# Reading the moving operand backwards and the weights in steps of two, in a two-layer decoder trunk

## The chip, the core and the metric

The kernel runs on one core of one Trainium2 chip. The metric is the device time of one execution in microseconds. Before the change two runs gave 976.68 and 978.26 us, with a median of 977.47 us.

## What is computed

The reference is a decoder trunk of two layers over 256 tokens of width 1024, in float32. Cut to what matters here:

```python
def swiglu(h, w_in, w_out):
    g, u = jnp.split(h @ w_in, 2, axis=-1)
    return (jax.nn.silu(g) * u) @ w_out

for layer in range(2):
    if layer == 1:
        k_sh, v_sh, F_sh = shared_kv(x, ...)              # h @ kv_w, gates
    sh1, sc1, g1, sh2, sc2, g2, sh3, sc3, g3 = split(c_act @ ada_w[layer] + ada_b[layer], 9)
    h = modulate(rms_norm(x, norm_g[layer, 0]), sh1, sc1)
    x = x + 0.5 * g1 * swiglu(h, ffn_w_in[layer, 0], ffn_w_out[layer, 0])
    h = modulate(rms_norm(x, norm_g[layer, 1]), sh2, sc2)
    mix = diff_attention(h, ...) if layer == 0 else forgetting_attention(h, ..., k_sh, v_sh, F_sh)
    x = x + g2 * mix
    h = modulate(rms_norm(x, norm_g[layer, 2]), sh3, sc3)
    x = x + 0.5 * g3 * swiglu(h, ffn_w_in[layer, 1], ffn_w_out[layer, 1])
return rms_norm(x, final_g)
```

A feed-forward block takes the 256 tokens through 2 x 2816 hidden columns and back. There are four of these blocks, and they hold most of the arithmetic; the two attentions, their projections and one shared key and value projection hold the rest.

## The kernel before, in words

Activations are kept transposed: a tile has 128 features on the partitions and the 256 tokens along the free axis. Every large product is made in a split form. A float32 operand is written as a high part of type float32r (tiles `HH`, `hidh`, `wh`) and a low part, the rest (tiles `HL`, `hidl`, `wl`). The helper `mm3` then issues three TensorE matmuls into one PSUM sum: high weights with high activations, low weights with high activations, high weights with low activations. In `mm3` the weight block of 128x128 is the **stationary** operand, which TensorE loads ahead of the matmul, and the activations of 256 tokens are the **moving** operand, which it streams. So each matmul has a weight load of its own, and writes 256 columns of float32 into PSUM. Where a bias column rides along, a matmul has 258 columns.

Weights arrive from HBM as a stream of pieces of up to 1024 columns. SyncE issues a DMA into a `raw` tile, ScalarE copies it to `wh`, VectorE subtracts to get `wl`. A piece of 1024 columns holds eight blocks, that is 24 matmuls. `take` hands out the pieces in order, and its inner `blk(c, w)` gives the two views, high and low, of the block that starts at column `c`.

Names of the products that go through `mm3`: `pf`, `pg`, `pu` (into a feed-forward block; in the first block, four of its eleven column groups are `pf`), `po` (out of it), `pqk`, `pk` (query and key projections), `pw` (attention output), and with 258 columns `lp`, `lg`, `lu`, `lq` (the first products after a new residual, whose normalisation is applied later). Not through `mm3` go: the value projections `pv`, where the weights are the moving operand with 512 columns and the activations are stationary; the last feed-forward output, also called `po`, where weights of 256 columns move and `hidh` or `hidl` is stationary; the forget gate `pzf`; and the small float32 products and transposes of the attention.

The order of instructions on every engine is fixed when the program is built. `InOrder` wraps each engine, keeps an estimate of when each tile is ready, and the background work (ScalarE copies, VectorE subtractions, and the VectorE reductions of the `ada` matrices) is put in where that estimate leaves room. The estimate knows a tile by its name and, for some tiles, by the offset of the view.

One detail of the weight tiles matters below. `wh` and `wl` are 1088 columns wide, and a table `shift` makes a few pieces begin 16 or 32 columns (64 or 128 bytes) later in their tile: the first piece of one group of products in each feed-forward block, and all pieces of the last output projection. All others begin at column 0.

Of the kernel before, what the change touches and what calls it, by code (L numbers as in the profile page):

```python
# [17 lines left out]
P = 128  # L18
D = 1024
S = 256  # L20
NC = D // P
HD = 64
AH = 8
# [27 lines left out]
V_ADAB = 65  # L51


class InOrder:


# [18 lines left out]
    def __getattr__(self, name):  # L75
        f = getattr(self.engine, name)

        def call(*args, **kw):
            aps = [v for v in (*args, *kw.values()) if hasattr(v, "tensor")]
            if aps:  # L80
                names = [(v.tensor.name, v.offset if v.tensor.name[:2] in ("HH", "HL", "x_", "mo") else 0) for v in aps]
                cost = self.fixed + self.rate * math.prod(aps[0].shape[1:])
                if aps[1:] and aps[1].dtype == F32:
                    cost *= {"matmul": 4, "transpose": 2}.get(name, 1)
                start = max(InOrder.ready.get(n, 0.0) for n in names[name == "matmul":])
                if self.fill and not self.busy:
                    self.busy = True
                    self.fill(start)
                    self.busy = False
                self.t = max(self.t, start) + cost  # L90
                if name == "dma_start":
                    InOrder.ready[names[0]] = self.t + 2.0
                else:
                    outs = [names[0]] + ([(kw["accum_out"].tensor.name, 0)] if kw.get("accum_out") is not None else [])
                    for n in outs:
                        InOrder.ready[n] = self.t + 0.06
            else:
                self.t += 1.3
            return self.tc.keep_in_program_order(f(*args, **kw))  # L99
        return call  # L100
# [3 lines left out]
def trunk(ctx, tc, a, out):  # L104
# [125 lines left out]
    stream = []  # L230
# [4 lines left out]
    def add_ffn(l, i):  # L235
        if (l, i) == (0, 0):
            stream.extend((a["win0"][k], K0 * 512, 1024) for k in range(NC))
        n = 2 * (NG - K0 if (l, i) == (0, 0) else NG)
        stream.extend((a["win"][win0_of(l, i) + u], 2048, 1024) for u in range(n))
        if (l, i) == (1, 1):  # L240
            for u in range(4):
                stream.extend((a["wlast"][u, :, c:c + n], n, step)
                              for c, n, step in ((0, 2048, 1024), (2048, 2048, 1024), (4096, 1536, 768)))
        else:
            stream.extend((a["wout"][(2 * l + i) * 16 + u], 11 * P, 768) for u in range(16))
# [11 lines left out]
    stream += [(a["wo"][u], 2048, 1024) for u in range(4, 8)]  # L257
    add_ffn(1, 1)

    pieces = [(src, c0, min(step, ncols - c0), c0 + step >= ncols)  # L260
              for src, ncols, step in stream for c0 in range(0, ncols, step)]

    shift = {}
    for (l, i), j in ((0, 0), K0), ((0, 1), 1), ((1, 0), 0), ((1, 1), 1):
# [7 lines left out]
    raws, his, los = [], [], []  # L272
# [52 lines left out]
    def take(src, split=False):  # L325

        u = taken[0]
        assert stream[u][0].tensor.name.endswith(src), (stream[u][0].tensor.name, src)
        p0 = done[0] = begun[0]
        while len(used) < p0:  # L330
            used.append(pe.t)
        while len(his) < p0 + 2:
            cp_part()
        while len(los) < p0 + 2:
            sub_part()
        taken[0] += 1
        begun[0] += 2
        step = stream[u][2]

        def blk(c, w=P):  # L340
            o = c % step
            if c >= step and not split and done[0] == p0:
                done[0] = p0 + 1
                used.append(pe.t)
            return his[p0 + c // step][:, o:o + w], los[p0 + c // step][:, o:o + w]
        return blk

    def work(cols):

        credit[0] = min(CREDIT, credit[0] + pace[0] * 2 * cols / 2048)  # L350
        if mode[0] != "hold":
            bg()
# [51 lines left out]

    def mm3(ps, w, xx, first, last):
        (wh, wl), (xh, xl) = w, xx
        mm(ps, wh, xh, start=first, stop=False, skip_group_check=True)
        mm(ps, wl, xh, start=False, stop=False, skip_group_check=True)
        mm(ps, wh, xl, start=False, stop=last, skip_group_check=True)
        work(P)  # L410


    HH = cp_.tile([P, NC, SP_], F32R, name="HH")
    HL = cp_.tile([P, NC, SP_], F32R, name="HL")
# [492 lines left out]
    for k in range(0, NC, 2):  # L907
# [3 lines left out]
        if k % 4:  # L911
            i = k // 4
# [481 lines left out]
def _layout(x, c, ada_w, ada_b, norm_g, ffn_w_in, ffn_w_out, a_w_qkv, a_w_o, a_lambda,  # L1394
            a_subln_g, rel_bias, kv_ada_w, kv_ada_b, kv_norm_g, kv_w, fgate_w, fgate_b,
            b_w_q, b_w_o, final_g):
    cat = np.concatenate
    r = {}
    r["x"] = x[0].T.reshape(NC, P, S).transpose(1, 0, 2)
    r["c"] = c.reshape(1, D)  # L1400

    def cols(v):
        return v.reshape(-1, P).T

    def pairs(m):
        m = m.reshape(-1, P, D)
        return m

    ada, adab = [], []

    def unit(b0, b1, v0, v1):
        ada.append(cat([b0, b1], axis=1))
        adab.extend([v0, v1])

    def ada_sec(wT, bb, sec):
        return wT[sec * D:(sec + 1) * D].reshape(NC, P, D), bb[sec * D:(sec + 1) * D].reshape(NC, P)

    def mod_pair(wT, bb, s_sc, s_sh):
        w1, b1 = ada_sec(wT, bb, s_sc)
        w0, b0 = ada_sec(wT, bb, s_sh)  # L1420
        for j in range(NC):
            unit(w1[j], w0[j], b1[j], b0[j])

    for l in range(2):
        if l == 1:
            mod_pair(kv_ada_w.T, kv_ada_b, 1, 0)
        wT = ada_w[l].T
        for s in range(3):
            mod_pair(wT, ada_b[l], 3 * s + 1, 3 * s)
            w, b = ada_sec(wT, ada_b[l], 3 * s + 2)  # L1430
            for j in range(0, NC, 2):
                unit(w[j], w[j + 1], b[j], b[j + 1])
    r["ada"] = np.stack(ada)
    r["vecs"] = cat([cols(norm_g), cols(kv_norm_g), cols(final_g), cols(a_subln_g), np.stack(adab, axis=1)], axis=1)

    def gu(w):
        g = w[:, :FF].reshape(NC, P, NG, 256)
        u = w[:, FF:].reshape(NC, P, NG, 256)
        return cat([g, u], axis=3)

    win = []
    for l in range(2):
        for i in range(2):
            w = gu(ffn_w_in[l, i])
            if (l, i) == (0, 0):
                r["win0"] = w[:, :, :K0].reshape(NC, P, K0 * 512)
                w = w[:, :, K0:]
            n = w.shape[2]
            win.append(w.reshape(2, 4, P, n, 512).transpose(3, 0, 2, 1, 4).reshape(2 * n, P, 2048))
    r["win"] = cat(win, axis=0)  # L1450
    w = ffn_w_out.reshape(4, FF, D)
    r["wout"] = w[:3].reshape(3, 2, 11, P, NC, P).transpose(0, 4, 1, 3, 2, 5).reshape(48, P, 11 * P)
    r["wlast"] = w[3].reshape(22, P, 4, 256).transpose(2, 1, 0, 3).reshape(4, P, 22 * 256)
    r["fin"] = final_g.reshape(1, D)

    def vmat(w):
        return w.reshape(2, 4, P, 2, 512).transpose(3, 0, 2, 1, 4).reshape(4, P, 2048)

    def kouter(w):
        return w.reshape(4, 2, P, D).transpose(0, 2, 1, 3).reshape(4, P, 2048)  # L1460

    def bpairs(w):
        return w.reshape(NC, P, 4, 256).transpose(2, 1, 0, 3).reshape(4, P, 2048)

    w = a_w_qkv[0]
    qk = cat([w[:, :D].reshape(NC, P, AH, P), w[:, D:2 * D].reshape(NC, P, AH, P)], axis=3)
    r["wqk"] = qk.transpose(2, 1, 0, 3).reshape(AH, P, 2048)
    r["wv"] = vmat(w[:, 2 * D:])
    r["wo"] = cat([kouter(a_w_o[0]), kouter(b_w_o[0])], axis=0)
    r["wkk"] = bpairs(kv_w[:, :D])  # L1470
    r["wkv"] = vmat(kv_w[:, D:])
    r["wq"] = bpairs(b_w_q[0])
    r["fgw"] = fgate_w.reshape(NC, P, BH).transpose(1, 0, 2)
    r["fgb"] = fgate_b.reshape(BH, 1)
    k = _constants()

    def rows(v):
        return np.concatenate([v, np.zeros((P - v.shape[0], v.shape[1]), np.float32)], axis=0)

    r["misc"] = cat([k["ident"], k["cmask"], k["ub"], rows(k["hot"]),  # L1480
                     np.broadcast_to(k["umask"], (P, 383)), rows(rel_bias),
                     np.broadcast_to(a_lambda.reshape(1, 4 * HD), (P, 4 * HD))], axis=1)
    return {k: np.ascontiguousarray(v) for k, v in r.items()}
# [16 lines left out]
```

## Time and profile before

| | before |
|---|---|
| runs | 976.68 and 978.26 us, median 977.47 us |
| span of the profiled execution, first to last instruction | 974.4 us |
| TensorE matmuls | busy 963.7 us, 8124 of them |
| TensorE weight loads | busy 939.9 us, 8124 of them |
| VectorE | busy 818.5 us |
| ScalarE | busy 552.4 us |
| HBM read | 264.75 MB, 274 GB/s over the span |

The span lies 3.07 us under the median of the runs: 2.3 to 3.9 us of a run are outside the first and the last instruction. Of the rows, two readings need care. The busy time of one matmul, 276 ns at 256 columns, is not what it costs: matmuls are pipelined, and the next one starts long before. What a matmul costs in a row of them is the distance between starts, which follows from the length of an unbroken piece of the chain divided by its count. And a weight load runs while the matmul before it streams, so the two TensorE rows lie on top of each other.

### The profile page before, as it was taken

To read this page: it belongs to the slowest core of one execution; us is meant where nothing else is said; L and a number is where in the kernel's file an instruction comes from. 1 tells how busy PE (TensorE), PEld (TensorE's weight loads), DVE (VectorE), ACT (ScalarE), POOL (GpSimd) and SP (SyncE) were. 2 spreads that over 40 slices of the span, in tenths; PEclk is the share of its full clock that TensorE was granted. 3 is DMA by queue.
4 is the path that set the end of the run, shared out by engine and by line. 5 is a ranking of instruction groups with operands and counts; after the bars stand their busy time and mean duration, and the time that the engine had idled before them with its cause. 6 is when DMAs were issued, how large, how long until landed. Compare 5 with 4: busy or idle time off the path is not lost.

```text
span 974.4 us, 20491 instructions
## 1 busy us (share of the span) xinstructions
PE 963.7 (99%) x8124; PEld 939.9 (96%) x8124; DVE 818.5 (84%) x1372; ACT 552.4 (57%) x902; POOL 54.6 (6%) x94
## 2 busy tenths in 40 slices
PE   8999999999999999999999999999999999999997
PEld 6999999998999999999997999999998999999997
DVE  7989979989999999878899989989977699555575
ACT  5466545566787645455576554445567576455432
POOL 0000200000112000000000000000011014300000
PEclk9999999999999999999999999999999999999999
DMA  9988999967776699888959899998885337978651
GB/s 360 415 352 279 332 372 339 345 225 272 293 239 232 209 381 370 293 287 314 329 179 370 308 338 337 345 314 319 297 278 174 104 109 228 266 149 276 185 152 44
DMA packets 69473, 268.22 MB, mean 275 GB/s; under 512 B 9417, under 2 KB 10225, under 8 KB 59266
## 3 DMA queue, kind: packets, MB, share of 16 engines
q1 hardware_dynamic: 66016, 259.69, 76.1%
q0 software_dynamic: 3072, 6.92, 2.5%
q8 instruction: 63, 1.03, 0.4%
q10 hardware_dynamic: 290, 0.32, 0.1%
q14 instruction: 32, 0.26, 0.1%
HBM read 264.75 MB, written 2.66 MB: 274 GB/s over the span
## 4 chain that ended last, share of the span: by engine, by line
PE 97%; DVE 1%; DMA 1%; ACT 0%; issue 0%; SPq 0%; DVEq 0%; ACTq 0%
PE po L99 25%; PE pg L99 21%; PE pu L99 21%; PE pf L99 5%; PE pv L99 5%; PE pw L99 4%; PE lp L99 4%; PE pqk L99 3%; PE wb L99 1%; PE lq L99 1%; PE lu L99 1%; PE lg L99 1%; PE pk L99 1%; PE sb L99 1%; DMA ada<-in_ada 1%; PE s L99 1%
## 5 line engine op out<-in xcount | busy, mean ns | idle before, releaser
L99 ACT CAST wh<-raw 128x1024 fp32r<-128x1024 f32 (+1 forms) x360 | 347.3, 975 | 210.8 <-PE pu L99 82.0
L99 DVE TENSOR_TENSOR wl<-raw,wh 128x1024 fp32r<-128x1024 f32 (+1 forms) x360 | 398.6, 1126 | 70.9 <-ACT sg L99 20.3
L99 DVE CUSTOM_DVE_ANT_0 ada<-ada,cact,vecs 128x1024 f32<-128x1024 f32 x160 | 203.6, 1279 | 0.4 <-DMA ada<-in_ada 0.4
L99 PE MATMUL pg<-HH,wh 128*128 128x256 f32 x608 | 168.0, 276 | 0.0
L99 PE MATMUL pg<-HH,wl 128*128 128x256 f32 x608 | 167.9, 276 | 0.0
L99 PE MATMUL pu<-HH,wh 128*128 128x256 f32 x608 | 167.9, 276 | 0.0
L99 PE MATMUL pu<-HL,wh 128*128 128x256 f32 x608 | 167.9, 276 | 0.0
L99 PE MATMUL pg<-HL,wh 128*128 128x256 f32 x608 | 167.9, 276 | 0.0
L99 PE MATMUL pu<-HH,wl 128*128 128x256 f32 x608 | 167.9, 276 | 0.0
L99 PE MATMUL po<-hidh,wh 128*128 128x256 f32 x528 | 145.7, 276 | 0.0
L99 PE MATMUL po<-hidh,wl 128*128 128x256 f32 x528 | 145.7, 276 | 0.0
L99 PE MATMUL po<-hidl,wh 128*128 128x256 f32 x528 | 145.7, 276 | 0.0
L99 PEld LDWEIGHTS pg<-HH,wh 128*128 128x128 f32 x608 | 114.1, 188 | 0.7 <-issue 0.6
L99 PEld LDWEIGHTS pg<-HH,wl 128*128 128x128 f32 x608 | 114.1, 188 | 0.0
L99 PEld LDWEIGHTS pu<-HH,wh 128*128 128x128 f32 x608 | 114.1, 188 | 0.0
L99 PEld LDWEIGHTS pg<-HL,wh 128*128 128x128 f32 x608 | 114.1, 188 | 0.0
L99 PEld LDWEIGHTS pu<-HL,wh 128*128 128x128 f32 x608 | 114.1, 188 | 0.0
L99 PEld LDWEIGHTS pu<-HH,wl 128*128 128x128 f32 x608 | 114.1, 188 | 0.0
L99 PEld LDWEIGHTS po<-hidh,wh 128*128 128x128 f32 x528 | 99.1, 188 | 0.0
L99 PEld LDWEIGHTS po<-hidl,wh 128*128 128x128 f32 x528 | 99.1, 188 | 0.0
L99 PEld LDWEIGHTS po<-hidh,wl 128*128 128x128 f32 x528 | 99.1, 188 | 0.0
L99 ACT CAST hidh<-hf 128x512 fp32r<-128x512 f32 x44 | 27.3, 621 | 40.5 <-DVE hf L99 40.4
(226 smaller groups left out, 1848.4 us busy)
## 6 DMA issues: line engine op xcount, KB each, us to landing
raw<-in_win SPq DMA_DIRECT2D x176, 512.0 KB, 6.8
ada<-in_ada SPq DMA_DIRECT2D x79, 1024.0 KB, 7.2
raw<-in_wout SPq DMA_DIRECT2D x48, 384.0 KB, 5.3
raw<-in_wout SPq DMA_DIRECT2D x48, 320.0 KB, 5.5
raw<-in_wqk SPq DMA_DIRECT2D x16, 512.0 KB, 5.8
raw<-in_wo SPq DMA_DIRECT2D x16, 512.0 KB, 5.8
raw<-in_wlast SPq DMA_DIRECT2D x16, 512.0 KB, 4.5
raw<-in_wv SPq DMA_DIRECT2D x8, 512.0 KB, 7.2
```

Of the source, the lines that this page charges most:

```text
L99: return self.tc.keep_in_program_order(f(*args, **kw))
```

## The change

`mm3` turns three views around: the moving operand, high and low, is read from the last column to the first, and the output is written from the last to the first, so each token's sum lands where it did. The stationary blocks of `mm3` are read with a step of two elements: on the host, pairs of neighbouring blocks of 128 columns are interleaved element by element, and `blk` hands out the even or the odd columns of a stretch of 256. Where a block has no partner in its piece (the last of eleven in each half of a `po` column, since 11 blocks are odd), it stays whole, with step one. Products outside `mm3` are as before, and so are the layouts of `wv`, `wkv` and `wlast`. `lowest` keeps the estimator's names of turned views equal to those of the plain ones.

```diff
+def lowest(v):
+    return v.offset + sum(step * (n - 1) for step, n in v.ap[1:] if step < 0)
+
+def turned(v):
+    return v[:, ::-1]
...
+    stream = [(src, ncols, step, lambda i, n=ncols, s=step: min(s, n - i * s)) for src, ncols, step in stream]
...
         def blk(c, w=P):
             o = c % step
...
+            if w == P:
+                o, n = o // 256 * 256, o // P % 2
+                if o + 256 <= stream[u][3](c // step):
+                    return tuple(t[p0 + c // step][:, o + n:o + 256:2] for t in (his, los))
+                o += n * P
             return his[p0 + c // step][:, o:o + w], los[p0 + c // step][:, o:o + w]
...
     def mm3(ps, w, xx, first, last):
         (wh, wl), (xh, xl) = w, xx
+        ps, xh, xl = turned(ps), turned(xh), turned(xl)
         mm(ps, wh, xh, start=first, stop=False, skip_group_check=True)
         mm(ps, wl, xh, start=False, stop=False, skip_group_check=True)
         mm(ps, wh, xl, start=False, stop=last, skip_group_check=True)
...
+    def mixed(w):
+        return np.swapaxes(w.reshape(w.shape[:-1] + (w.shape[-1] // 256, 2, P)), -1, -2).reshape(w.shape)
...
-        return cat([g, u], axis=3)
+        return mixed(cat([g, u], axis=3))
...
-    r["wqk"] = qk.transpose(2, 1, 0, 3).reshape(AH, P, 2048)
+    r["wqk"] = mixed(qk.transpose(2, 1, 0, 3).reshape(AH, P, 2048))
```

The other layouts that `mm3` uses (`win`, `wout`, `wo`, `wkk`, `wq`) are wrapped in `mixed` in the same way.

No instruction moves: on all five engines the instructions stand in the same order with the same shapes, before and after. One thing differs on TensorE. Sixteen matmuls, each the first that writes a PSUM bank after a phase of other products, now wait for TensorE's own count as well, which names an earlier writer of that bank. The first place is the second pair of `lp` banks after the first feed-forward block. Before:

```order
L99 MATMUL lp_2570<-HL,wh 128x258
L99 MATMUL lp_2640<-HH,wh 128x258
L99 MATMUL lp_2640<-HH,wl 128x258
L99 MATMUL lp_2640<-HL,wh 128x258
L99 MATMUL lp_2641<-HH,wh 128x258
```

After:

```order
L109 MATMUL lp_2570<-HL,wh 128x258
L109 MATMUL lp_2640<-HH,wh 128x258 [waits PE_49]
L109 MATMUL lp_2640<-HH,wl 128x258
L109 MATMUL lp_2640<-HL,wh 128x258
L109 MATMUL lp_2641<-HH,wh 128x258 [waits PE_49]
```

The count that such a wait asks for is that of a matmul at least 51 places earlier on TensorE.

More of the change, by code (lines that the diff above doesn't have):

```diff
@@ L80, in call @@
             if aps:
-                names = [(v.tensor.name, v.offset if v.tensor.name[:2] in ("HH", "HL", "x_", "mo") else 0) for v in aps]
+                names = [(v.tensor.name, lowest(v) if v.tensor.name[:2] in ("HH", "HL", "x_", "mo") else 0) for v in aps]
                 cost = self.fixed + self.rate * math.prod(aps[0].shape[1:])
@@ L258, in trunk @@
     add_ffn(1, 1)
+    stream = [(src, ncols, step, lambda i, n=ncols, s=step: min(s, n - i * s)) for src, ncols, step in stream]
     pieces = [(src, c0, min(step, ncols - c0), c0 + step >= ncols)
-              for src, ncols, step in stream for c0 in range(0, ncols, step)]
+              for src, ncols, step, _ in stream for c0 in range(0, ncols, step)]
     shift = {}
@@ L1451, in _layout @@
     w = ffn_w_out.reshape(4, FF, D)
-    r["wout"] = w[:3].reshape(3, 2, 11, P, NC, P).transpose(0, 4, 1, 3, 2, 5).reshape(48, P, 11 * P)
+    w3 = w[:3].reshape(3, 2, 11, P, NC, P).transpose(0, 4, 1, 3, 2, 5).reshape(48, P, 11 * P)
+    r["wout"] = cat([mixed(w3[:, :, :10 * P]), w3[:, :, 10 * P:]], axis=2)
     r["wlast"] = w[3].reshape(22, P, 4, 256).transpose(2, 1, 0, 3).reshape(4, P, 22 * 256)
@@ L1459, in kouter @@
     def kouter(w):
-        return w.reshape(4, 2, P, D).transpose(0, 2, 1, 3).reshape(4, P, 2048)
+        return mixed(w.reshape(4, 2, P, D).transpose(0, 2, 1, 3).reshape(4, P, 2048))
     def bpairs(w):
-        return w.reshape(NC, P, 4, 256).transpose(2, 1, 0, 3).reshape(4, P, 2048)
+        return mixed(w.reshape(NC, P, 4, 256).transpose(2, 1, 0, 3).reshape(4, P, 2048))
     w = a_w_qkv[0]
     qk = cat([w[:, :D].reshape(NC, P, AH, P), w[:, D:2 * D].reshape(NC, P, AH, P)], axis=3)
-    r["wqk"] = qk.transpose(2, 1, 0, 3).reshape(AH, P, 2048)
+    r["wqk"] = mixed(qk.transpose(2, 1, 0, 3).reshape(AH, P, 2048))
     r["wv"] = vmat(w[:, 2 * D:])
```

## The prediction

> **What bounds the kernel now.** I read the page first: which engine is busy for the whole span, and whether its clock is held back.
>
> ```profile
> PE 963.7 (99%) x8124; PEld 939.9 (96%) x8124; DVE 818.5 (84%) x1372; ACT 552.4 (57%) x902; POOL 54.6 (6%) x94
> PEclk9999999999999999999999999999999999999999
> PE 97%; DVE 1%; DMA 1%; ACT 0%; issue 0%; SPq 0%; DVEq 0%; ACTq 0%
> ```
>
> TensorE is never without work, its granted clock is full in all slices, and 97% of the chain that ended last is TensorE. The view of waits says the same from the other side: the longest wait of TensorE for another engine is this.
>
> ```profile
> PE pf L99 <- ACT HH L99: 1.9, 1, 1.9
> ```
>
> So the time is the number of matmuls times the distance between their starts, and a change of access patterns can act only on that distance. I read it from the chain in order of time, where unbroken rows of matmuls stand with start, length and count.
>
> ```profile
> 137.96 59.84 PE po L99 x528
> 201.13 8.70 PE lp L99 x72
> 209.82 5.50 PE pv L99 x24
> 299.05 7.55 PE pw L99 x64
> 499.43 10.90 PE pk L99 x96
> 778.78 8.29 PE pw L99 x72
> 908.04 59.99 PE po L99 x528
> ```
>
> Dividing: `po` 113.3 ns, `pk` 113.5, `pw` 115 to 118, all at 256 columns; `lp` 120.8 at 258 columns; `pv` 229 at 512. The last `po` (113.6) and `pv` do not pass through `mm3`. These are not one price per column: two columns more cost 7.5 ns, where 2/256 of 113.3 would be 0.9. The next rows, from the same view at two other places, are the ones that matter most.
>
> ```profile
> 62.84 0.71 PE pu L99 x6
> 66.29 0.68 PE pg L99 x6
> ...
> 799.82 0.72 PE pu L99 x6
> 801.95 0.68 PE pg L99 x6
> ```
>
> Six matmuls of the same shape, engine and clock take 0.71 or 0.72 us, and a few microseconds later 0.68: 118 to 120 ns against 113.3. The longer distance lasts from the start of `pg` until about the place where the one piece with the 64-byte shift has been used, both times. Nothing else on the engine differs there, so the place of the weights in their tile decides between two distances. I read this as two streams of TensorE, the weight load and the moving operand, that get into each other's way in SBUF, with a pattern that locks.
>
> **The change, part by part.** Moved: no instruction on any engine and no DMA; the interleaving is made in the layout on the host, so ScalarE, VectorE and the queues handle the same tiles of the same sizes. The terms are the matmuls in `mm3`, counted from the groups (each row is one of three or six alike):
>
> ```profile
> L99 PE MATMUL pg<-HH,wh 128*128 128x256 f32 x608 | 168.0, 276 | 0.0
> L99 PE MATMUL po<-hidh,wh 128*128 128x256 f32 x528 | 145.7, 276 | 0.0
> L99 PE MATMUL pf<-HH,wh 128*128 128x256 f32 x128 | 35.8, 280 | 1.9 <-ACT HH L99 1.9
> L99 PE MATMUL lp<-HH,wh 128*128 128x258 f32 x96 | 27.8, 289 | 0.0
> L99 PE MATMUL pqk<-HH,wh 128*128 128x256 f32 x96 | 27.0, 282 | 0.0
> L99 PE MATMUL pw<-obh,wh 128*128 128x256 f32 x64 | 18.4, 288 | 0.0
> L99 PE MATMUL lg<-HH,wh 128*128 128x258 f32 x32 | 9.4, 295 | 0.0
> ...
> L99 PEld LDWEIGHTS pg<-HH,wh 128*128 128x128 f32 x608 | 114.1, 188 | 0.7 <-issue 0.6
> ```
>
> That is `pg` and `pu` 6 x 608 = 3648, `po` 1584, `pf` 384, `pqk` 288, `pw` 384, `pk` 3 x 32 = 96, and with 258 columns `lp` 288 and `lg`, `lu`, `lq` 96 each, 576. In all 6960 of 8124; the 144 of `po` without a partner block keep their step of one.
>
> What the new distance is, no row shows, since nothing in this trace reads backwards or with a step on TensorE. The bounds come from the nearest rows. Above stands the locked state that hurts, 118 to 121 ns. Below, the rows with the least distance that still pair each weight load of 128 columns with a stream, the float32 transposes:
>
> ```profile
> 745.14 0.44 PE wa L99 x4
> 745.59 0.22 PE wb L99 x2
> ```
>
> That is 110 ns a piece; by the rounding of 0.22 it could be 107.5 to 112.5. In the change, the weight stream strides 8 bytes per column instead of 4 and the moving stream runs the other way, so their relative walk through SBUF is a new one. If a weight column is read every second moving column (128 columns beside 256, both taking about a matmul's distance), the step of two gives both streams the same speed in bytes: 1024 bytes each per matmul, where before it was 512 against 1024. Two streams of the same speed and the same order of addresses would keep their distance, and after one collision stay clear of each other; whether the load takes its columns from the last to the first, as the turned stream does, no row tells. I take **110 ns** for 256 columns, and 110 x 258/256 = 110.9 for 258, because a pair of load and stream at that distance is in the trace.
>
> The sum, against 974.4: `pg` and `pu` 3648 x (113.5 - 110) = 12.8, with 113.5 as 0.68/6 and some groups at 0.71; `po` 1584 x 3.3 = 5.2; `pqk` and `pk` 384 x 3.5 = 1.3; `pw` 384 x 5 = 1.9 at 115; the 576 wide ones x (120.8 - 110.9) = 5.7. For `pf` I take nothing: its stage is held by something else, below. Total 26.9, so 947.5 in the span, and with the 3.07 us by which the median of the runs lies above this span, **950.5 us**.
>
> [...]
>
> What would be late next if TensorE gains 3%: these are stretches with busy time of each engine, clock, DMA share and GB/s.
>
> ```profile
> 24.00:68.00 44.00, 43.98 (x372) 43.29 (x371) 42.70 (x64) 25.17 (x32) 0.00 (x0) 1.00 1.01 406
> 222.00:300.00 78.00, 77.07 (x616) 70.95 (x615) 73.89 (x180) 55.71 (x155) 8.46 (x13) 1.00 0.76 270
> 545.00:666.00 121.00, 121.00 (x1070) 121.00 (x1069) 107.42 (x143) 60.26 (x72) 0.00 (x0) 1.00 0.93 334
> ```
>
> In `pf` (24 to 68) DMA is busy throughout at 406 GB/s and VectorE 97%: no gain there, and no loss while the distance stays under the 44.0/372 = 118 ns of that stretch. In the feed-forward stretch from 545, VectorE is 89% busy and DMA moves 334 GB/s; 3% faster asks for 92% and 344 GB/s, under what the `pf` stage reaches. In the attention from 222, VectorE at 73.9 of 78 us leaves 4 us, and my sum takes about 2 from it (288 x 3.5 and half of the `pw`). So the cover holds, barely; without it, 1 to 3 us of the gain are lost. The sixteen added waits cost nothing: each asks for a matmul at least 51 places back, 51 x 113 ns = 5.8 us, and is met before it is asked.
>
> **The rivals.** (1) *The distance stays at 113.3*: the stream of float32r itself runs at that rate, whatever the weights do. For it: the value is exact in 59.84 us of `po` and at many addresses, and `pv` with half as many loads per column has 229, just over twice as much. Against it: the step from 0.71 to 0.68. [...] Only the wide ones could then move, 576 x at most 6.6 = 3.8: 973 to 978.
>
> (2) *The new pattern locks at the longer distance.* The place is every `mm3` matmul outside `pf`; the price is 118 instead of 113.3, 5328 x 4.6 for `pg`, `pu`, `po` and `pk`, 672 x 3 for `pqk` and `pw`, nothing on the wide ones, which are in such a state already: 26.5 us, so 1004. If they go as far as the wide ones are now, 120.8 x 256/258 = 119.9, it is 5328 x 6.5 + 672 x 5 = 38.0, so 1016. It turns the sign once the mean over the 6576 outside `pf` is above today's 114.2, and is over 2% from 19.5/6576 = 3 ns more. For it: three different distances are in this trace already, and the kernel's shifts were placed for the old pattern.
>
> (3) *One of the two accesses is served at half rate*: a load that reads 128 columns out of twice as many bytes, or a PSUM write in falling order. Then each matmul costs about what `pv` does with twice the columns, 229: 6960 x 115 = 800 us more, about 1775. [...]
>
> (4) *The change does less than it says*, since 144 `po` keep their step: these are 2%, too few for a case.
>
> **How the numbers follow.** Forecast, 940 to 958: 0.50. A distance under 109, below 940: 0.04. Rival 1, with gains that stay under 2%: 0.20. Rival 2: 0.18, most of it from 1004 to 1016. Rival 3: 0.08. The range is 934 to 1016: its low end is 107.5 ns (6576 x 2.5 = 16.4 under the forecast), its high end takes in rival 2 at both its prices; rival 3, what lies under 934 and a lock worse than any in this trace stay out, with 0.15 or so. The likeliest case alone is 940 to 958. 2%, or 19.5 us, is about what a measurement of this kernel can tell from no change: faster 0.54, within 0.20, slower 0.26.
>
> **What the profile after would show.** If I am right, the long `po` piece of 59.84 us is 58.1, six `pg` take 0.66 or less from the first group on, without a second state, 72 `lp` take 8.0; `pv` (5.50 for 24) and the last `po` (59.99) are unchanged, a control on the same chip; the clock row stays at 9, VectorE's share rises to 86 or 87%. If 0.68 stays at 0.68, rival 1; if it is 0.71 or more, rival 2; if the 276 ns of a matmul and the 188 of a load grow by 100, rival 3. I am wrong, with the mechanism right, if TensorE begins to wait for `wl` or `wh` in the waits.

## The result: 1001.7 us, slower by 2.5%

Two runs of the changed kernel gave 1001.56 and 1001.87 us, median 1001.71, against 977.47 before: the ratio is 1.025 with a 95% interval of 1.0221 to 1.028. The profiled execution spans 999.8 us, 25.4 more than before. The forecast was 950.5; the time is that of rival 2 (1004), inside the range of 934 to 1016, on the other side of zero.

The page of the changed kernel, in the rows that answer to those shown of before:

```profile
PE 990.4 (99%) x8124; PEld 967.6 (97%) x8124; DVE 820.8 (82%) x1372; ACT 554.1 (55%) x902; POOL 55.1 (6%) x94
PEclk9999999999999999999999999999999999999999
PE 97%; DVE 1%; ACT 1%; issue 0%; DVEq 0%; ACTq 0%
```

TensorE is still 97% of the chain, its granted clock is still full (0.998 over the span), and the count of matmuls is the same, so I look for the time in the distance between them. The chain in order of time shows by how much (start, length, piece, count):

```profile
142.05 62.19 PE po L109 x528
207.55 8.64 PE lp L109 x72
216.19 5.51 PE pv L109 x24
305.98 7.81 PE pw L109 x64
512.95 11.31 PE pk L109 x96
933.33 60.04 PE po L109 x528
```

Before and after, `po` went from 113.3 to 117.8 ns, `pk` from 113.5 to 117.8, `pw` from 118 to 122; `lp`, with 258 columns, from 120.8 to 120.0. The two that do not pass through `mm3`, `pv` (5.51 for 24) and the last `po` (60.04 for 528), stayed where they were (5.50 and 59.99 before). The place at which `pg` had two distances before now has one:

```profile
61.96 0.71 PE pg L109 x6
...
71.15 0.71 PE pu L109 x6
```

So the sum closes: `pg` and `pu` 3648 x (117.8 - 113.5) = 15.7, `po` 1584 x 4.45 = 7.0, `pk` 0.4, `pqk` and `pw` about 1.5, `pf` about 0.9 with the gaps between its pieces, the wide ones (258 columns) a little less than before (-0.5): 25.0 of 25.4 us.

### The profile page after: what moved, and what is told of

It reads as the page before. It is cut to its first block, busy times and chain, and to the rows that moved or that the text cites. A ratio compares the mean times of both kernels' runs of the same rounds, so it can differ in the third digit from the quotient of the medians.

```text
span 999.8 us, 20496 instructions
## 1 busy us (share of the span) xinstructions
PE 990.4 (99%) x8124; PEld 967.6 (97%) x8124; DVE 820.8 (82%) x1372; ACT 554.1 (55%) x902; POOL 55.1 (6%) x94
## 4 chain that ended last, share of the span: by engine, by line
PE 97%; DVE 1%; ACT 1%; issue 0%; DVEq 0%; ACTq 0%
PE po L109 25%; PE pg L109 22%; PE pu L109 21%; PE pf L109 5%; PE pv L109 4%; PE pw L109 4%; PE lp L109 3%; PE pqk L109 3%; PE wb L109 1%; PE lq L109 1%; PE lu L109 1%; PE lg L109 1%; PE pk L109 1%; PE sb L109 1%; PE s L109 1%; PE psn L109 1%
## 5 line engine op out<-in xcount | busy, mean ns | idle before, releaser
L109 PE MATMUL pu<-HL,wh 128*128 128x256 f32 x608 | 171.5, 282 | 0.0
L109 PE MATMUL pg<-HL,wh 128*128 128x256 f32 x608 | 171.5, 282 | 0.0
L109 PE MATMUL pu<-HH,wl 128*128 128x256 f32 x608 | 171.5, 282 | 0.0
L109 PE MATMUL pg<-HH,wl 128*128 128x256 f32 x608 | 171.5, 282 | 0.0
L109 PEld LDWEIGHTS pg<-HH,wh 128*128 128x128 f32 x608 | 118.0, 194 | 0.7 <-issue 0.6
L109 PEld LDWEIGHTS pu<-HH,wh 128*128 128x128 f32 x608 | 118.0, 194 | 0.0
L109 PEld LDWEIGHTS pg<-HH,wl 128*128 128x128 f32 x608 | 117.4, 193 | 0.0
L109 PEld LDWEIGHTS pu<-HL,wh 128*128 128x128 f32 x608 | 117.4, 193 | 0.0
L109 PEld LDWEIGHTS pg<-HL,wh 128*128 128x128 f32 x608 | 117.4, 193 | 0.0
L109 PE MATMUL po<-wl,hidh 128*128 128x256 f32 x176 | 48.7, 276 | 0.0
```

## The experiments

### One half of the change at a time, in the trunk

The expectations set three theories against each other. In theory A the weight load and the moving stream collide in SBUF, and their relative walk sets the distance. In theory B the falling write to PSUM costs. In theory C the weight load with a step of two costs.

`two_only` is the changed kernel with the views not turned:

```diff
-        ps, xh, xl = turned(ps), turned(xh), turned(xl)
```

> The changed kernel without the turned views: weights with a step of two, moving operand and output forward as before. Theory A: a pattern of its own, at 113.3 or another locked distance, anywhere from 950 to 1005 us. Theory B (falling PSUM writes cost): as before the change, 977 us, with po at 113.3. Theory C (the step of two costs): as after the change, 1002 us, with po at 117.8.

Measured: 1015.83 us, ratio 1.037 (1.0311 to 1.0427). The step of two alone is worse than the whole change, and worse than any of the three theories gave.

```profile
142.62 63.23 PE po L109 x528
518.59 11.52 PE pk L109 x96
945.14 62.21 PE po L109 x528
```

`po` is at 119.8 ns. The last row is the output projection that the change leaves alone: it went from 113.6 to 117.8 here, with the same instructions on the same tiles as before, and it keeps that distance through all 528 matmuls. Before the change its first 24 had 118.6, and from the third 24 on all had 113.3. So the same row of matmuls has two steady distances. Its own addresses do not decide between them; I put it down to what ran ahead of it. That is the part of theory A that held.

`rev_only` has the turned views and the old layout:

```diff
     def mixed(w):
-        return np.swapaxes(w.reshape(w.shape[:-1] + (w.shape[-1] // 256, 2, P)), -1, -2).reshape(w.shape)
+        return w
...
-            if w == P:
-                o, n = o // 256 * 256, o // P % 2
-                if o + 256 <= stream[u][3](c // step):
-                    return tuple(t[p0 + c // step][:, o + n:o + 256:2] for t in (his, los))
-                o += n * P
```

> The changed kernel without the mixing: weights with a step of one in the old layout, moving operand and output turned. Theory A: a locked distance that may differ from both, 950 to 1005 us. Theory B: as after the change, 1002 us, po at 117.8. Theory C: as before the change, 977 us, po at 113.3.

Measured: 1000.94 us, ratio 1.0213 (1.0145 to 1.028). Turning alone gives the whole loss. The interval is wide and reaches below 2%, since one of the seven runs of before took 988.87 us; `mov_only`, further down, gives the same loss with a narrow one.

```profile
141.87 62.19 PE po L109 x528
512.92 11.31 PE pk L109 x96
933.28 60.04 PE po L109 x528
```

Each half costs by itself, and the costs do not add: `po` is at 119.8 and 117.8 apart, and at 117.8 together. None of the three theories said that.

### Patterns without the trunk

To see the patterns themselves I wrote a kernel of matmuls alone: 48 in a row for each pattern, in the order of `mm3`, four repeats of the whole list. Its core:

```python
CASES = [("fwd", 1, 1, 1, 256, 0), ("rev", -1, 1, -1, 256, 0), ("fwdtwo", 1, 2, 1, 256, 0), ...]
# name, step of the moving operand, of the weights, of the output, columns, shift of the weights
for j in range(48):
    x, w = (hh, hh, hl)[j % 3], (wh, wl, wh)[j % 3]
    nc.tensor.matmul(o, run(w, c, P, ws), run(x, 0, n, ms), ...)
```

> A kernel of matmuls alone, in the split form's order (three per block, float32r, 48 in a row), with one access pattern per group and four repeats at other phases; its output is a copy of x, not the trunk. Theory A (the weight load and the moving stream collide in SBUF, and their relative walk sets the distance): forward is 113.3 or 117.8 ns depending on the phase, reversed with step two 117.8; with the moving operand held still (step zero) or the weights held still the distance falls to about 109; the direction of the output alone changes nothing. Theory B (writing PSUM in falling order is what costs): only the groups with a falling output are at 117.8, whatever the two reads do, and a still operand changes nothing. Theory C (the load with a step of two is what costs): all groups with step two are at 117.8 or more, those with step one at 113.3, and step four is worse still.

The chain over the second repeat and the start of the third; a piece divided by its 48 is the distance:

```profile
152.74 5.68 PE revx L82 x48
175.62 5.75 PE revoutx L82 x48
192.91 5.36 PE stillx L82 x48
198.27 5.45 PE wstillx L82 x48
203.72 5.36 PE bothstillx L82 x48
209.08 11.21 PE fourx L82 x48
231.49 5.46 PE shiftbx L82 x48
242.63 5.65 PE revtwoshiftax L82 x48
253.94 10.93 PE widex L82 x48
264.87 11.21 PE widerevx L82 x48
276.08 5.38 PE narrowx L82 x48
281.46 5.74 PE fwdx L82 x48
```

Read them in pairs. A row's rounding is worth 0.1 ns per matmul. With the moving operand held at one address (`still`) the distance is 111.7, with the weights at one address as well (`bothstill`) it is the same, and with 240 moving columns (`narrow`) it is 112.1. So fewer columns, or one address in place of a stream, save next to nothing below that: I read 111.7 as the **floor of the weight load** at a step of one. By `bothstill` the addresses do not set it at this step; a least distance of any pair of load and matmul would look the same. With the weights held at one address (`wstill`) a forward stream of 256 columns takes 113.5 over the whole row and 113.3 after its first few, and with 512 columns and moving weights (`wide`) 227.7 and 226.9: the **stream has a floor at 113.3**. Before the change the kernel stood on that floor. `shiftb`, weights 64 bytes further, stands on it too, where `fwd` is at 119.6: that is the interference, and it comes on top of the floor. At the place where `fwd` has 119.6, a turned stream (`rev`) has 118.3, so there the price of turning does not show at all; with the weights 16 bytes further, the change's own pattern (`revtwoshifta`) is at 117.7, as in the trunk. A backward stream of 512 columns takes 233.5 (`widerev`). A weight load with a step of four takes 233.5 as well (`four`). `revout`, with the output alone turned, says nothing yet, since `fwd` beside it is at 119.6 too.

Theory A missed here: with an operand held still the distance did not fall to 109 but to 111.7 or 113.5. And theory C's order is there, but not its shape, since step four is not a little worse but double.

### The floors one by one

The second kernel of this kind held one side still and looked for relative places. The list of cases is the edit:

```python
("revwstill", -1, 0, -1, 256, 0, 0), ("widestill", 0, 1, 1, 512, 0, 0), ("widewstill", 1, 0, 1, 512, 0, 0),
("widerevmov", -1, 1, 1, 512, 0, 0), ("widerevout", 1, 1, -1, 512, 0, 0), ("three", 1, 3, 1, 256, 0, 0), ...
# two more shifts per case at the end: of the weights, of the moving operand
```

> Matmuls alone again (split-form order, 48 in a row, float32r), twice each; the output is a copy of x, not the trunk. Theory D, formed from the first kernel of this kind: the distance is the largest of a floor of the weight load (111.8 ns) and a floor of the moving stream (113.3 for 256 columns forward, 116.7 backward), and the relative place of the two adds up to 7 ns on top. Then: backward with the weights held still 116.7, at 512 columns 233.3 with the output either way; 512 forward with the weights held still 226.7; a falling output with a forward read 226.7; a forward read with a step of two in the weights reaches 113.3 at some shift; backward never falls under 116.7 at any shift; 258 columns have a shift at which they fall from 120 to about 114.3. Rival, theory A (only the collision of the two streams costs, there is no floor of the stream): 512 columns with the weights held still fall to 216 or less, backward with the weights held still equals forward, and backward reaches 113.3 or less at some shift.

```profile
19.07 5.65 PE revwstillx L103 x48
24.72 10.40 PE widestillx L103 x48
35.12 11.10 PE widewstillx L103 x48
46.22 11.20 PE widerevwstillx L103 x48
57.42 11.20 PE widerevmovx L103 x48
68.63 10.90 PE widerevoutx L103 x48
79.53 11.20 PE widetwox L103 x48
102.01 8.27 PE threex L103 x48
161.53 5.90 PE fwdshbx L103 x48
190.29 5.65 PE revshax L103 x48
236.32 5.70 PE biasshfx L103 x48
242.02 5.60 PE biaswstillx L103 x48
276.90 5.44 PE movshcx L103 x48
```

Backward with the weights still is 117.7 at 256 columns and 233.3 at 512, and with moving weights (`widerevmov`) 233.3 again. At three shifts of the weights the backward distance was 117.7, 117.7 and 119.8. In all three kernels of this kind no backward row came under 117.7 at 256 columns or under 233.3 at 512, whatever the weights did, where forward rows came down to 113.3 (`movshc`) and 227.1 (`widerevout`). I read that as a floor of the backward stream. It is not proof that no collision is in it, since weights held at one address are still loaded (the page of the next kernel has 96 loads for the 96 matmuls of `slimwstill`): forward with 512 columns they gave 231.2 (`widewstill`), more than the 227.1 with moving weights. The row `widerevout` (227.1) is a forward read with a falling output and costs what forward costs (`wide`, 227.7). A weight load with a step of three is at 172. Forward reaches 113.3 at a relative place of 64 bytes from either side (`shiftb` for the weights, `movshc`, 5.44, for the moving operand).

The expectation failed in four details. `fwdtwo` did not come down to 113.3 at any of six shifts (118.7 to 120.7). With 258 columns the best place gave 118.7, though with the weights still they take 116.7. Forward with 512 columns and the weights still was 231.2, not 226.7. And the relative place of the two operands adds more than 7 ns: `fwdshb`, weights 48 bytes further, is at 122.9 against 113.3. One row that the expectation did not price goes against a distance that is the larger of two floors: `widetwo`, a forward stream of 512 columns with a weight load of step two, takes 233.3, though the same stream reaches 227.1 with a step of one (`widerevout`), and a load of step two takes 117.7 beside an operand at one address (`stilltwo`, in the next kernel), half of that.

The third kernel put each floor alone:

```python
("slimone", 1, 1, 1, 64, 0, 0), ("slimtwo", 1, 2, 1, 64, 0, 0), ...,
("wideline", "lines", 0, 1, 512, 0, 0), ("movpairs", "pairs", 0, 1, 256, 0, 0), ("stilltwo", 0, 2, 1, 256, 0, 0), ...
# "lines": four elements forward, then the four ahead of them; "pairs": two of every four elements
```

> Matmuls alone (split-form order, 48 in a row, float32r), twice each; the output is a copy of x, not the trunk. Each floor by itself. [...] Theory E (a step other than one costs by its elements, not by lines): step two with 64 columns is at 223 or stays at 111.8, two of every four elements is at 113, and lines read forward inside are at 226.7. For 258 columns: if a relative place of the operands exists that clears them, one of the eight shifts falls to 116.7.

```profile
46.18 11.18 PE slimfourx L92 x48
101.16 11.20 PE widelinex L92 x48
112.36 11.09 PE movpairsx L92 x48
123.45 5.65 PE stilltwox L92 x48
129.10 5.66 PE wstilltwobackx L92 x48
```

Here both halves of the change stand alone, and they are the same number within the rounding. `stilltwo` is a weight load with a step of two beside a moving operand that reads one address: 117.7. `wstilltwoback` is a backward stream beside weights that read one address: 117.9. Stretches of 16 bytes taken from the last to the first (`wideline`) cost 233.3 at 512 columns although the elements inside go forward, and two of every four elements (`movpairs`) cost 231, about as much as twice the columns in a row. So in these rows the price goes by stretches of at least 16 bytes and by their order, not by the element. Whether the unit is larger than 16 bytes no run tells, since no step above four was tried.

The rows with 64 columns can't be used for the floors at full speed: in them the granted clock fell to half (0.50 in the first line), and the row of the clock on the page shows the fall both times round.

```profile
40.00:50.00 10.00, 10.00 (x47) 0.50 0.01 2
160.00:170.00 10.00, 10.00 (x86) 1.00 0.01 2
PEclk9965555558999999999997555555699999999999
```

But they add one thing. `slimfour` has 233 ns at the halved clock, and `four` had 233.5 at the full one, so in these two rows the load's price at a step of four does not follow TensorE's clock.

### Back in the trunk: output and moving operand apart

`out_only` and `mov_only` are `rev_only` with one turned view or the other:

```diff
-        ps, xh, xl = turned(ps), turned(xh), turned(xl)
+        ps = turned(ps)                      # out_only
+        xh, xl = turned(xh), turned(xl)      # mov_only
```

> The turned output alone in the trunk: moving operand forward, weights with a step of one in the old layout, only the PSUM view turned, so the tokens of each product land in reverse and the later values differ. Theory D: no cost, 975 to 980 us, po at 113.3. Theory B (falling PSUM writes cost): 1001 us, po at 117.8.

> The turned moving operand alone in the trunk: output forward, weights with a step of one in the old layout; the tokens of each product land in reverse and the later values differ. Theory D: 998 to 1003 us, po at 117 to 118, and never under 116.7. Theory B: 977 us, po at 113.3. Theory A (only the collision costs): anywhere from 950 to 1005.

Measured: `out_only` 976.86 us, ratio 1.0005 (0.9995 to 1.0015); `mov_only` 1001.47 us, ratio 1.0255 (1.024 to 1.0271). The first row is of the former, the second of the latter:

```profile
137.94 59.84 PE po L109 x528
...
140.91 62.19 PE po L109 x528
```

The falling write to PSUM is free to within 0.15%, and theory B falls: of the three turned views, the moving operand read backwards makes the whole loss. The long `po` has 59.84 us with the falling output and 59.84 before the change. The step of the weights has a price of another shape: a step of four is at 233.5, about twice the 117.7 of a step of two, and a step of two already pays against the 111.7 of a step of one.

## Why the prediction was wrong

**The bound** was read rightly: TensorE's chain, a full clock, a time that is count times distance. The counts hold, and VectorE fell to 82% as the span grew. The added waits cost nothing: `out_only` has them too (902 matmuls with a wait in its trace, against 885 before) and takes 976.86 us. `pf`, put at nothing, gave 0.9 us of loss.

**The step that failed** is "I take **110 ns** for 256 columns ... because a pair of load and stream at that distance is in the trace". The row was one of float32 transposes with 128 moving columns, another type and another size. For float32r the load alone has 111.7 (`still`), and a forward stream of 256 columns 113.3 (`wstill`, `movshc`), so the distance of before had nothing left to lose. The gain of 3.3 to 3.5 ns per matmul, the largest terms of the sum, became a loss of 4.3 to 4.5. The step from 0.71 to 0.68, which I took for proof that 113.3 held a collision too, showed only that 118 did. Rival 1 had that right ("the stream of float32r itself runs at that rate"), and its evidence was in the prediction: `pv` at 229 for 512 columns is just over twice 113.3, with half as many loads. What rival 1 did not see is that turning has a price of its own.

**The equal speeds** were the other part of it: "Two streams of the same speed and the same order of addresses would keep their distance". Whether the load goes from back to front no run shows by itself; its price at a step of two, equal to that of a backward stream, fits it. But both accesses that made the speeds equal have a price. Either of them, over the same 1024 bytes, takes 117.7 ns beside an operand that reads one address. In the trunk the two together take 117.8, the larger of the two and not their sum, and so the halves do not add.

**Rival 2** had the size (26.5 us against 24.2 between the medians), the place and the sign, with 0.18. Its reason is not the one that the runs show. A row of matmuls can indeed stay at a longer distance, as the last projection of `two_only` does. But the turned kernel needs no such lock: the backward stream is at 117.7 with the weights still, and no arrangement of the weights that I tried brought it under that. Rival 2 was priced from a row, 118, that happened to lie next to this floor; that the size fits is luck.

**Rival 3**, half rate, did not come true for the step of two. At a step of three the load is at 172 and at four at 233.5, so the price comes in by degrees. Of the wide ones I expected 8.0 us for 72 `lp`; they gave 8.64 after 8.70.

**What stays open.** With a step of two and a forward stream the distance lies above the larger floor: 119.8 in `two_only`, and 233.3 in `widetwo` against 227.1 in `widerevout`. For 258 columns the best of fourteen relative places was 118.7 against 116.7 with the weights still, and one of these places (`biasmixb`) had 118.8 the first time round and 122.2 the second, with the same instructions. I take all of this for interference of the kind that the 64 bytes remove at 256 columns, but that is not shown, and the rule for it was not found. No version that beats the kernel before came out of this: on more than 5000 matmuls it stands on the stream's floor, and the wide ones could give, as an estimate, at most 576 x 4 ns = 2.3 us, 0.2%. No such version was run.

## What to carry to other kernels

Before hoping to lower a distance, look for its floor: hold one operand at one address and see what is left, at more than one relative place. If the kernel already stands on that floor, as this one did at 113.3, a pattern can only add: here it added 4.3 to 4.5 ns. Let the moving operand run forward (113.3 against 117.7 backward, at 256 columns) and the weights be contiguous (111.7 at a step of one, 117.7 at two, 172 at three, 233.5 at four). Stretches of 16 bytes in falling order cost what a backward stream costs (`wideline`, 233.3 at 512 columns); the direction in which the output is written was free here (976.86 against 976.74 us). A row of another data type and another number of columns is not a floor for yours: the float32 transposes of 128 columns had 110, the float32r rows of 256 columns came down to 113.3.

## What had not been expected of the hardware

- A stream read from back to front is slower than forward: 233.3 (`widerevmov`) against 227.1 ns (`widerevout`) for 512 columns of float32r, and 216.7 (`widestill`, 10.40 for 48) when the moving operand is one address.
- With a weight load of 128 float32r columns per matmul, the distance is 111.7 ns at step one and 117.7 at two beside a moving operand at one address, and 172 at three and 233.5 at four beside a forward stream of 256 columns. So the step counts from two on.
- In the rows with 64 columns per matmul the granted clock fell to 0.50 (`m3_single_floors`, 40 to 50 us), though TensorE was busy 10 of 10 us.
- The relative place of weights and moving operand is worth up to 10 ns on 113 (`fwdshb`, 122.9, against `movshc`, 113.3), and its effect seems to outlast the instructions that caused it: in `two_only` the last output projection, itself unchanged, went from 113.6 to 117.8.
